# A decoder trunk on one core: group 0's values in two passes, compression adds on GpSimd, another order of blocks, maxima ahead of exponentials

## The chip, the core and the metric

The kernel runs on one core of a Trainium2 chip. Its engines are TensorE (PE, with PEld for its weight loads), VectorE (DVE), ScalarE (ACT), GpSimd (POOL) and SyncE (SP), which issues the DMAs. The metric is the device time of one execution in microseconds (us); lower is better. The times of the kernel before are 1174.12, 1171.5 and 1175.63, median 1174.12.

## What is computed

A trunk of two layers over 512 tokens of width 1024, in f32. Layer 1 is a retention layer, followed by a gated per-layer embedding. From its output one norm and one projection give the keys and values that layer 2 attends to, and a small MLP compresses 32 tokens at a time to one compressed key and value per group. Layer 2 is attention of 16 query heads in four groups: over the compressed positions (31 of them), over selected blocks and over a window. With 512 tokens the selection takes every block and the window covers all, so these two are full causal attentions. The three results are mixed by sigmoid gates, multiplied by a SiLU gate and projected.

```python
def compress_blocks(a, pe, w1, w2):
    sub = a.reshape(b, g, t // CMP_STRIDE, CMP_STRIDE, d)
    blocks = jnp.concatenate([sub[:, :, o:o + n_cmp] for o in range(lc)], axis=3)
    blocks = (blocks + pe).reshape(b, g, n_cmp, CMP_LEN * d)
    return jax.nn.gelu(blocks @ w1) @ w2
...
    s_c = jnp.einsum('bgrqd,bgnd->bgrqn', q, k_cmp) * scale
    p_c = jnp.where(valid_c, jax.nn.softmax(jnp.where(valid_c, s_c, NEG), axis=-1), 0.0)
...
    return gates[..., 0:1] * o_c + gates[..., 1:2] * o_s + gates[..., 2:3] * o_w
```

## The kernel before

Every f32 product is made of three matmuls on rounded operands: each operand is split into a high half (a ScalarE copy to the rounded type) and a low half (a VectorE subtraction), and `mm3` issues high x high, high x low and low x high. The schedule is written by hand: each engine executes its instructions in the order in which the code issues them, and the framework adds only the waits. A tile of PSUM that two engines use is handed over in that order too.

**Weights** come as a stream of pieces (class `Stream`), in the order that `order()` writes out, through four raw buffers and six slots for split pieces. `low` (L205) makes the low half of the oldest piece on VectorE and then issues on SP the DMA that reuses its raw buffer, four pieces ahead. `high` (L190) makes a high half on ScalarE when a slot is free. `mul` (L176) multiplies norm gains into a raw piece on GpSimd, two instructions for each q or k piece and none for the pieces of the compression weights (wk, wv). `tick` does low, high, mul once or twice, and is called from all over the kernel; `get` makes sure that the next piece is ready, and `done` frees its slot.

**Start.** 24 matmuls on zeros (L327) run ahead of the first projection, whose first operands come from ScalarE L136 and L389 and VectorE L137 and L390.

**Group 0's values.** `v_proj(0, t)` multiplies the normed rows of token tile t with three pieces (`kvb`, together 8 k-steps of 304 columns) into one PSUM bank and splits the result into v2H and v2L; the last 48 columns become the branch gates. The four tiles go one after the other, with the transposes of the last row block (`to_aT(3)`) between the second and the third.

**Compression.** `compress(b)`, b = 0 for keys and 1 for values, is a generator. `block(s)`, for s = 0 to 7, adds the position embedding to every 16th column of the projected `ckv` (L783, VectorE, 4 x 4 x 31 elements a partition, read with a step of 16), copies the result to a high half (L785, ScalarE), ticks (for s > 1), and makes the low half (L788, VectorE). Step s multiplies blocks s with one piece of wk or wv (12 matmuls of 256 columns) and then issues block(s + 2). After step 7 come a Gelu, two transposes with a split, and the second layer (w2). Compression of the keys is interleaved with the projections c_proj(1, g), that of the values with the query projections `q_proj(0, h)`: two steps after each of the first three queries, then steps 6 and 7 in a row, then the fourth query. The first key projection, the w2 layer of the values, the first scores and the second key projection follow (L1012 to L1019).

**Scores.** `scores(g, u)` serves unit u of a group (u = 2h for selection, 2h + 1 for the window, of head h). It fills three PSUM banks, for row block 3, row block 2 and row blocks 0 and 1; per bank VectorE adds the causal mask and then, per row block, takes the maximum (L944), after which ScalarE takes the exponential with a running sum (L945). In even units the compressed positions' scores stand in the same banks; `cmp_probs` adds their mask (L883) after all banks and goes on with their softmax. Between units `pair_tile` adds output tiles to the residual (L1006) and `probs_T` transposes probabilities and splits them (L364, L365).

Of the kernel before, what the change touches and what calls it, by code (L numbers as in the profile page):

```python
# [47 lines left out]
def order():  # L48
# [26 lines left out]
    def kk(g):  # L75
        return [("kv", 0, 1024, b + 128 * g, 128) for b in (1024, 1536)]
# [4 lines left out]
    def q(g):  # L81
        return [("nin", 0, 1024, 512 * g + 128 * h, 128) for h in range(4)]
# [6 lines left out]
    for n, dense in (("wk", [("kv", 0, 1024, 512 + 128 * g, 128) for g in range(4)]),  # L89
                     ("wv", q(0)[:3])):  # L90
        o += [("w2", 0, 512, 0, 128)] if n == "wv" else []
        for i, d in enumerate(dense):
            o += [d] + [(n, 512 * (2 * i + e), 512, 0, 256) for e in (0, 1)]
    o += [("wv", 512 * i, 512, 0, 256) for i in (6, 7)] + [q(0)[3]] + kk(0)
# [142 lines left out]
def decoder(ctx: ExitStack, tc: tile.TileContext, x, xT, stream, cst, msk, gains, fnorm, out):  # L237
# [88 lines left out]
    for i in range(24):  # L326
        pe.matmul(o[:, :256], masks[:, :128], masks[:, :256], start=True, stop=True)  # L327
# [146 lines left out]
    def run(g):  # L474
        for _ in g:
            pass
# [228 lines left out]
    def v_proj(g, t, p, bank="d", tick=True):  # L705
        n = 256 if g else 304
        o = psum(bank)[:, :n]
        k0 = 0
        for q in p:
            m = q.h.shape[1]  # L710
            mm3(o, [(aH[:, t, k0 + k], aL[:, t, k0 + k], q.h[:, k], q.l[:, k])
                    for k in range(m)], k0 == 0, k0 + m == NK)
            k0 += m
        split_psum(v2H[:, t], v2L[:, t], o[:, :256])
        if g == 0:
            act.activation(bg[:, t], o[:, 256:], AF.Tanh, scale=0.5)
        if tick:
            W.tick()
        if t == 3:
            for q in p:  # L720
                q.done()
# [53 lines left out]
    def compress(b):  # L775

        def block(s):
# [5 lines left out]
            dve.tensor_add(B[:, :, :, :31], src,  # L783
                           pos[:, :, None, None].to_broadcast([128, 4, 4, 31]))
# [54 lines left out]
    v_proj(0, 0, p, "d", False)  # L839
    v_proj(0, 1, p, "o", False)  # L840
    to_aT(3, hn[1])
    v_proj(0, 2, p, "d", False)
    W.tick(1)
    v_proj(0, 3, p, "s")
# [13 lines left out]
    for h in range(3):  # L858
        f = q_proj(0, h)
        next(f)  # L860
        if h < 2:
            next(comp)
        run(f)
        next(comp1)
        next(comp1)
    next(comp1)
    next(comp1)
    f = q_proj(0, 3)
    next(f)
    act.activation(small[:, 250:251], half, AF.Exp)  # L870
    next(comp1)
    run(f)
# [6 lines left out]
    def cmp_probs(g, h, banks):  # L879

        q, q4 = pc[h % 2], pc4[h % 2]
        for i, o in banks:
            dve.tensor_add(q[:, i:i + 2], o, cmask[:, i:i + 2])  # L883
# [24 lines left out]
    def scores(g, u):  # L908
# [4 lines left out]
        cmp = []  # L913
# [5 lines left out]
        for bank in ((3,), (2,), (0, 1)):  # L919
# [8 lines left out]
            if e and 2 in bank:  # L928
                block(o[:, 416:448], 3, 0, 32)
                cmp.append((2, o[:, 0:448].rearrange("p (a n) -> p a n", a=14)[:, 0:14:13]))  # L930
            elif e and 0 in bank:
                cmp.append((0, o[:, 0:480].rearrange("p (a n) -> p a n", a=3)[:, 0:2, :32]))
# [8 lines left out]
            for i, f in zip(bank, at):  # L941
                n = 128 * i + 128
                w = o[:, f:f + n]
                dve.reduce_max(mx[:, i:i + 1], w, axis=mybir.AxisListType.X, negate=True)  # L944
                act.activation(Pu[:, PO[i]:PO[i] + n], w, AF.Exp, bias=mx[:, i:i + 1],  # L945
                               accum_out=sm_[:, i:i + 1])
        chain = cmp_probs(g, h, cmp) if e else iter(())
# [63 lines left out]

    k_proj(0, 0)  # L1012
    next(comp1)
    w2p.done()
    dve.tensor_scalar(bg, bg, 0.5, 0.5, op0=OP.mult, op1=OP.add)
    sums, chain = scores(0, 0)
    scale_probs(0, 0, sums)
    run(chain)
    k_proj(0, 1)  # L1019
# [155 lines left out]
```

## Time and profile before

| | |
|---|---|
| median of the three runs | 1174.12 us |
| the profiled execution, its own time | 1176.46 us |
| its span, first to last instruction | 1174.7 us |
| mean granted TensorE clock | 0.988 |
| busy: PE, PEld | 1140.1 us, 970.0 us |
| busy: DVE, ACT, POOL | 727.8, 490.8, 294.9 us |
| HBM read, written | 98.83 MB, 2.10 MB |

Busy time says how much of the span an engine worked; an idle engine that nobody waits for costs nothing. [...] In a timeline a line stands for a run of like instructions, and the brackets hold the engine's idle time ahead of it and the instruction that ended this.

### The profile page before, as it was taken

Reading aid. Unit: us, or ns where it says so; the run is one execution under the profiler, and the core shown is the slowest. Engines: PE = TensorE matmul, PEld = TensorE weight load, DVE = VectorE, ACT = ScalarE, POOL = GpSimd, SP = SyncE. Lnnn points to the kernel's source line nnn. Section 1 sums busy time; section 2 is a strip of 40 time slices with the busy share of each in tenths; the row PEclk is TensorE's granted clock in tenths of the full one; section 3 lists DMA queues with packets and bytes.
Section 4 is the critical chain, followed back from the end, with each engine's and each line's share of the span. In section 5 each row is a group of like instructions: output and inputs, shape, how many; then the busy total and the mean of one; then the engine's idle time right before and its main releaser. Section 6 shows DMA issues by size and latency. Waiting matters only on the chain. (4 is left out here: it accounts for less than half of the span.)

```text
span 1174.7 us, 15278 instructions
## 1 busy us (share of the span) xinstructions
PE 1140.1 (97%) x5806; PEld 970.0 (83%) x5806; DVE 727.8 (62%) x1242; ACT 490.8 (42%) x916; POOL 294.9 (25%) x341
## 2 busy tenths in 40 slices
PE   8999999999999999899699999999999999999997
PEld 7888888888888888888587888888898888887886
DVE  4746336544534556467857764778468774787555
ACT  6333233232323445345446443444344533444653
POOL 0212003002100222223435331454243431321012
PEclk9999999999999999999799999999999999999999
DMA  8422321322232131255512201221121211221211
GB/s 326 141 97 72 111 96 54 93 95 72 90 108 90 54 124 39 83 152 175 149 69 73 73 21 51 73 74 56 50 91 54 73 54 41 86 77 50 72 37 71
DMA packets 29593, 101.90 MB, mean 87 GB/s; under 512 B 3536, under 2 KB 3792, under 8 KB 29520
## 3 DMA queue, kind: packets, MB, share of 16 engines
q1 hardware_dynamic: 29088, 100.15, 26.2%
q8 instruction: 45, 0.74, 0.3%
q10 hardware_dynamic: 432, 0.79, 0.2%
q14 instruction: 28, 0.23, 0.1%
HBM read 98.83 MB, written 2.10 MB: 86 GB/s over the span
## 5 line engine op out<-in xcount | busy, mean ns | idle before, releaser
L355 PE MATMUL d<-arenaR 128*128 128x512 f32 (+2 forms) x2904 | 678.1, 386 | 10.4 <-DVE arenaF L1006 3.6
L355 PEld LDWEIGHTS d<-arenaR 128*128 128x128 f32 x2904 | 525.6, 189 | 113.9 <-DVE arenaF L1006 5.5
L355 PE MATMUL s<-arenaR 128*128 128x512 f32 (+8 forms) x1182 | 239.5, 353 | 0.2 <-DVE arenaR L829 0.2
L205 DVE TENSOR_TENSOR arenaR<-arenaF,arenaR 128x1024 fp32r<-128x1024 f32 (+1 forms) x142 | 194.1, 1386 | 66.1 <-ACT arenaR L190 66.0
L355 PEld LDWEIGHTS s<-arenaR 128*128 128x128 f32 x1182 | 200.3, 188 | 29.8 <-DVE arenaR L829 0.3
L190 ACT ACTIVATE arenaR<-arenaF 128x1024 fp32r<-128x1024 f32 (+1 forms) x142 | 145.8, 1048 | 104.4 <-PE s L355 68.4
L176 POOL TENSOR_TENSOR arenaF<-arenaF 128x512 f32<-128x512 f32 x108 | 137.0, 1291 | 126.2 <-DMA arenaF<-stream_dram 126.1
L355 PE MATMUL o<-arenaR 128*128 128x512 f32 (+3 forms) x744 | 133.4, 331 | 11.0 <-DVE arenaR L788 5.0
L355 PEld LDWEIGHTS o<-arenaR 128*128 128x128 f32 x744 | 119.1, 198 | 24.0 <-DVE arenaR L788 5.8
L958 POOL TENSOR_SCALAR arenaF<-arenaF 128x512 f32<-128x512 f32 (+3 forms) x128 | 66.8, 541 | 254.1 <-ACT arenaR L364 120.1
L945 ACT ACTIVATE arenaF<-s,arenaF 128x512 f32<-128x512 f32 (+3 forms) x128 | 67.6, 528 | 102.9 <-DVE arenaF L944 100.2
L365 DVE TENSOR_TENSOR arenaR<-pt,arenaR 128x512 fp32r<-128x512 f32 (+1 forms) x141 | 82.8, 617 | 35.5 <-ACT arenaR L364 33.8
L364 ACT ACTIVATE arenaR<-pt 128x512 fp32r<-128x512 f32 (+1 forms) x141 | 70.7, 540 | 80.0 <-PE pt L967 40.4
L371 POOL TENSOR_TENSOR arenaF<-arenaF 128x1 f32<-128x1 f32 (+1 forms) x25 | 14.2, 568 | 294.7 <-DVE arenaF L370 294.7
L944 DVE TENSOR_REDUCE arenaF<-s 128x1 f32<-128x512 f32 (+3 forms) x128 | 62.9, 491 | 22.2 <-ACT arenaF L945 18.9
L355 PE MATMUL pt<-arenaR 128*128 128x512 f32 (+1 forms) x384 | 75.9, 349 | 0.0
L355 PEld LDWEIGHTS pt<-arenaR 128*128 128x128 f32 x384 | 62.7, 188 | 9.4
L209 DVE SCALAR_TENSOR_TENSOR arenaR<-arenaF,arenaR 128x512 fp32r<-128x512 f32 x64 | 45.7, 762 | 35.0 <-PE pt L355 21.4
L194 ACT ACTIVATE arenaR<-arenaF 128x512 fp32r<-128x512 f32 x64 | 43.1, 721 | 46.6 <-issue 22.3
L967 PEld LDWEIGHTS pt<-arenaF 128*128 128x128 f32 x318 | 38.4, 141 | 12.1 <-DVE arenaR L365 4.5
L967 PE MATMUL pt<-arenaF 128*128 128x128 f32 x318 | 45.1, 273 | 3.2 <-DVE arenaR L365 3.2
L1006 DVE TENSOR_TENSOR arenaF<-arenaF,d 128x512 f32<-128x512 f32 x64 | 41.8, 682 | 7.0 <-PE d L355 6.7
(126 smaller groups left out, 692.6 us busy)
## 6 DMA issues: line engine op xcount, KB each, us to landing
arenaF<-stream_dram SPq DMA_DIRECT2D x174, 512.0 KB, 3.5
arenaF<-xT_dram SPq DMA_DIRECT2D x8, 256.0 KB, 5.0
arenaF<-x_dram SPq DMA_DIRECT2D x4, 512.0 KB, 8.3
out_dram<-arenaF SPq DMA_DIRECT2D x3, 512.0 KB, 2.6
arenaF<-cst_dram SPq DMA_DIRECT2D x4, 256.0 KB, 3.8
arenaF<-stream_dram ACTq DMA_DIRECT2D x2, 256.0 KB, 4.4
arenaF<-stream_dram SPq DMA_DIRECT2D x2, 256.0 KB, 6.0
arenaF<-cst_dram SPq DMA_DIRECT2D x1, 512.0 KB, 9.9
```

What stands on the lines that cost most here:

```text
L176: self.nc.gpsimd.tensor_mul(r3[:, k], r3[:, k], g[:, k, None].to_broadcast([128, m // 2, w]))
L190: self.nc.scalar.activation(hi[:, :m * w], raw, AF.Copy)
L194: self.nc.scalar.activation(hi[:, c], raw[:, c], AF.Copy, scale=g[:, k:k + 1])
L205: self.nc.vector.tensor_sub(lo[:, :m * w], raw, hi[:, :m * w])
L209: self.nc.vector.scalar_tensor_tensor(lo[:, c], raw[:, c], g[:, k:k + 1], hi[:, c], op0=OP.mult, op1=OP.subtract)
L355: pe.matmul(o, a, b, start=start and i == 0, stop=stop and i == n - 1)
L364: act.activation(h, src, AF.Copy)
L365: dve.tensor_sub(l, src, h.bitcast(F32))
L944: dve.reduce_max(mx[:, i:i + 1], w, axis=mybir.AxisListType.X, negate=True)
L945: act.activation(Pu[:, PO[i]:PO[i] + n], w, AF.Exp, bias=mx[:, i:i + 1], accum_out=sm_[:, i:i + 1])
L958: pool.tensor_scalar(w, w, sm_[:, i:i + 1], 1.0, op0=OP.mult, op1=OP.mult)
L967: pe.transpose(p[:, f:f + 128], Pu[:, PO[i] + 128 * j:PO[i] + 128 * j + 128], ident)
```

## The change

Six edits, in the order of the diff:

- `order()` puts the fourth query piece, q(0)[3], between the sixth and the seventh wv piece, where it stood behind the eighth.
- The warm-up has 30 matmuls for 24.
- `v_proj` is divided: `v_sums` does the matmuls of given pieces into a given bank. Tiles 0, 1 and 2 of group 0 are first summed over pieces one and two, with the transposes of the last row block ahead of tile 2; then piece three is added to each and its result split; tile 3 comes last.
- The position add of `block(s)` is issued on GpSimd instead of VectorE.
- The driver of group 0 follows the new order of pieces: step 6 of the values' compression comes in the middle of the fourth query's projection and step 7 after it. The transposes follow the first key projection, the w2 layer follows the second, and the first scores stand between the two.
- In `scores` all maxima of a bank come ahead of its exponentials, and the add of the compressed positions' mask (earlier in `cmp_probs`) comes between them.

```diff
--- before.py
+++ after.py
@@ -87,11 +87,11 @@
     o += [("kvb", r, min(384, 1024 - r), 0, 304) for r in (0, 384, 768)]
     o += [("kv", 0, 1024, 128 * g, 128) for g in range(4)]
     for n, dense in (("wk", [("kv", 0, 1024, 512 + 128 * g, 128) for g in range(4)]),
-                     ("wv", q(0)[:3])):
+                     ("wv", q(0))):
         o += [("w2", 0, 512, 0, 128)] if n == "wv" else []
         for i, d in enumerate(dense):
             o += [d] + [(n, 512 * (2 * i + e), 512, 0, 256) for e in (0, 1)]
-    o += [("wv", 512 * i, 512, 0, 256) for i in (6, 7)] + [q(0)[3]] + kk(0)
+    o += kk(0)
 
     def block(kind, g, i):
         if kind == "emb":
@@ -323,7 +323,7 @@
 
     pool.memset(masks[:, :256], 0.0)
     o = psum("o")
-    for i in range(24):
+    for i in range(30):
         pe.matmul(o[:, :256], masks[:, :128], masks[:, :256], start=True, stop=True)
     for k in range(NK):
         nc.sync.dma_start(rx[:, k], xT[k // 2, :, 512 * (k % 2):512 * (k % 2) + 512])
@@ -702,15 +702,19 @@
     blk = [V(fb + 6144 + 512 * i, 512) for i in range(2)]
     hid = V(fb, 256)
 
-    def v_proj(g, t, p, bank="d", tick=True):
-        n = 256 if g else 304
-        o = psum(bank)[:, :n]
-        k0 = 0
+    def v_sums(t, o, p, k0):
         for q in p:
             m = q.h.shape[1]
             mm3(o, [(aH[:, t, k0 + k], aL[:, t, k0 + k], q.h[:, k], q.l[:, k])
                     for k in range(m)], k0 == 0, k0 + m == NK)
             k0 += m
+
+    def v_proj(g, t, p, bank="d", tick=True, o=None):
+        if o is None:
+            o = psum(bank)[:, :256]
+            v_sums(t, o, p, 0)
+        else:
+            v_sums(t, o, p[2:], 6)
         split_psum(v2H[:, t], v2L[:, t], o[:, :256])
         if g == 0:
             act.activation(bg[:, t], o[:, 256:], AF.Tanh, scale=0.5)
@@ -780,8 +784,8 @@
             src = bass.AP(tensor=src.tensor, offset=src.offset + 4 * s,
                           ap=[list(src.ap[0]), [1, 4], [512, 4], [16, 31]])
             pos = gn[:, (G_PEV if b else G_PEK) + 4 * s:][:, :4]
-            dve.tensor_add(B[:, :, :, :31], src,
-                           pos[:, :, None, None].to_broadcast([128, 4, 4, 31]))
+            pool.tensor_add(B[:, :, :, :31], src,
+                            pos[:, :, None, None].to_broadcast([128, 4, 4, 31]))
             act.activation(bkH[s % 4], blk[s % 2], AF.Copy)
             if s > 1:
                 W.tick()
@@ -836,12 +840,17 @@
     ple_gate(0, norm_rows, norm_T)
     p = v_pieces(0)
     W.tick(1)
-    v_proj(0, 0, p, "d", False)
-    v_proj(0, 1, p, "o", False)
+    o = [psum(bank)[:, :304] for bank in ("d", "o", "d", "s")]
+    v_sums(0, o[0], p[:2], 0)
+    v_sums(1, o[1], p[:2], 0)
     to_aT(3, hn[1])
-    v_proj(0, 2, p, "d", False)
+    v_sums(2, o[2], p[:2], 0)
+    v_proj(0, 0, p, tick=False, o=o[0])
+    v_proj(0, 1, p, tick=False, o=o[1])
     W.tick(1)
-    v_proj(0, 3, p, "s")
+    v_proj(0, 2, p, tick=False, o=o[2])
+    v_sums(3, o[3], p[:2], 0)
+    v_proj(0, 3, p, o=o[3])
     for i in range(2):
         dve.memset(blk[i], 0.0)
     for g in range(4):
@@ -855,32 +864,27 @@
     w2p = W.get("w2", 0, 512, 0, 128)
     comp1 = compress(1)
     next(comp1)
-    for h in range(3):
+    for h in range(4):
         f = q_proj(0, h)
         next(f)
         if h < 2:
             next(comp)
+        if h == 3:
+            next(comp1)
         run(f)
         next(comp1)
-        next(comp1)
-    next(comp1)
-    next(comp1)
-    f = q_proj(0, 3)
-    next(f)
+        if h < 3:
+            next(comp1)
     act.activation(small[:, 250:251], half, AF.Exp)
-    next(comp1)
-    run(f)
 
     tri = masks[:, M_TRI:M_TRI + 128]
     cmask = masks[:, M_CMP:M_CMP + 128].rearrange("p (i n) -> p i n", i=4)
     PO = [896, 1024, 512, 0]
     TO = [0, 512, 1024, 896]
 
-    def cmp_probs(g, h, banks):
+    def cmp_probs(g, h):
 
         q, q4 = pc[h % 2], pc4[h % 2]
-        for i, o in banks:
-            dve.tensor_add(q[:, i:i + 2], o, cmask[:, i:i + 2])
         mx, sm_ = scal(4), scal(4)
         dve.reduce_max(mx, q, axis=mybir.AxisListType.X)
         dve.tensor_sub(q, q, mx[:, :, None].to_broadcast([128, 4, 32]))
@@ -910,7 +914,6 @@
         Pu = P[u % 2]
         e = 0 if b else 32
         mx, sm_ = scal(4), scal(4)
-        cmp = []
 
         def block(w, i, lo, hi):
             c = slice(128 * i, 128 * i + 128)
@@ -927,9 +930,11 @@
                 f += n
             if e and 2 in bank:
                 block(o[:, 416:448], 3, 0, 32)
-                cmp.append((2, o[:, 0:448].rearrange("p (a n) -> p a n", a=14)[:, 0:14:13]))
+                cmp = 2, o[:, 0:448].rearrange("p (a n) -> p a n", a=14)[:, 0:14:13]
             elif e and 0 in bank:
-                cmp.append((0, o[:, 0:480].rearrange("p (a n) -> p a n", a=3)[:, 0:2, :32]))
+                cmp = 0, o[:, 0:480].rearrange("p (a n) -> p a n", a=3)[:, 0:2, :32]
+            else:
+                cmp = None
             if 1 in bank:
 
                 d = bass.AP(tensor=o.tensor, offset=o.offset + e,
@@ -939,12 +944,16 @@
                 d = o[:, at[0] + 128 * bank[0]:][:, :128]
                 dve.tensor_add(d, d, tri)
             for i, f in zip(bank, at):
+                dve.reduce_max(mx[:, i:i + 1], o[:, f:f + 128 * i + 128],
+                               axis=mybir.AxisListType.X, negate=True)
+            if cmp:
+                i, d = cmp
+                dve.tensor_add(pc[h % 2][:, i:i + 2], d, cmask[:, i:i + 2])
+            for i, f in zip(bank, at):
                 n = 128 * i + 128
-                w = o[:, f:f + n]
-                dve.reduce_max(mx[:, i:i + 1], w, axis=mybir.AxisListType.X, negate=True)
-                act.activation(Pu[:, PO[i]:PO[i] + n], w, AF.Exp, bias=mx[:, i:i + 1],
+                act.activation(Pu[:, PO[i]:PO[i] + n], o[:, f:f + n], AF.Exp, bias=mx[:, i:i + 1],
                                accum_out=sm_[:, i:i + 1])
-        chain = cmp_probs(g, h, cmp) if e else iter(())
+        chain = cmp_probs(g, h) if e else iter(())
         next(chain, 0)
         return sm_, chain
 
@@ -1009,14 +1018,15 @@
         for kind, *i in (b for h in range(4) for b in between(g, h)):
             yield from {"gate": g_proj, "q": q_proj, "nout": pair_tiles, "emb": emb_tiles}[kind](*i)
 
+    dve.tensor_scalar(bg, bg, 0.5, 0.5, op0=OP.mult, op1=OP.add)
     k_proj(0, 0)
     next(comp1)
-    w2p.done()
-    dve.tensor_scalar(bg, bg, 0.5, 0.5, op0=OP.mult, op1=OP.add)
     sums, chain = scores(0, 0)
     scale_probs(0, 0, sums)
+    k_proj(0, 1)
+    next(comp1)
+    w2p.done()
     run(chain)
-    k_proj(0, 1)
 
 
     PLAN = [3, 3, 2, 1, 2, 3, 2, 2]
```

## Rows read from the trace of the kernel before

**Rows 1.** Page, parts 1 and 6: busy us (share); issues, KB, us to landing
```profile
PE 1140.1 (97%) x5806; PEld 970.0 (83%) x5806; DVE 727.8 (62%) x1242; ACT 490.8 (42%) x916; POOL 294.9 (25%) x341
...
arenaF<-stream_dram SPq DMA_DIRECT2D x174, 512.0 KB, 3.5
```

**Rows 2.** Timeline, TensorE, start: start, us, instruction, count, [idle, releaser]
```profile
1.09 4.94 PE L327 MATMUL o<-masks 128*128 128x256 bf16 x24 [1.09 <-POOL masks L324]
7.94 13.19 PE L355 MATMUL d<-arenaR 128*128 128x512 f32 x48 [1.92 <-ACT arenaR L136]
20.97 11.04 PE L355 MATMUL s<-arenaR 128*128 128x512 f32 x48
```

**Rows 3.** Windows: stretch, length, busy us by engine, granted clock, DMA, GB/s
```profile
8.96:12.38 3.42, 3.42 (x9) 2.65 (x10) 3.42 (x6) 3.42 (x7) 0.00 (x0) 0.51 1.02 364
555.00:570.00 15.00, 13.90 (x82) 12.14 (x81) 12.12 (x14) 8.33 (x13) 1.84 (x2) 1.00 0.64 202
575.78:589.10 13.32, 8.93 (x31) 7.62 (x32) 9.99 (x7) 6.38 (x8) 9.93 (x8) 0.50 0.55 158
```

**Rows 4.** Timeline, TensorE, values of group 0
```profile
475.30 0.96 PE L355 MATMUL d<-arenaR 128*128 128x304 f32 x5 [3.35 <-DVE arenaR L205]
476.10 5.04 PE L355 MATMUL o<-arenaR 128*128 128x304 f32 x24
...
485.21 3.52 PE L355 MATMUL s<-arenaR 128*128 128x304 f32 x24
```

**Rows 5.** Timeline, VectorE, the same stretch
```profile
473.62 2.76 DVE L205 TENSOR_TENSOR arenaR<-arenaF,arenaR 128x608 fp32r<-128x608 f32 x2
```

**Rows 6.** Waits of TensorE: line, releaser, us in total, times, longest
```profile
PE o L355 <- DVE arenaR L788: 5.0, 3, 3.1
PE o L355 <- ACT arenaR L785: 4.7, 1, 4.7
PE d L355 <- DVE arenaF L1006: 3.6, 8, 0.9
...
PE o L355 <- DVE arenaR L365: 0.8, 1, 0.8
```

**Rows 7.** Timeline, TensorE, compression of the values
```profile
549.41 3.04 PE L355 MATMUL o<-arenaR 128*128 128x256 f32 x24
...
577.90 3.15 PE L355 MATMUL o<-arenaR 128*128 128x256 f32 x12 [0.80 <-DVE arenaR L788]
584.11 2.50 PE L355 MATMUL o<-arenaR 128*128 128x256 f32 x10 [3.06 <-DVE arenaR L788]
586.41 4.22 PE L355 MATMUL d<-arenaR 128*128 128x512 f32 x12
```

**Rows 8.** One line, L783: min/median/max ns, first and last start
```profile
L783 DVE TENSOR_TENSOR arenaF<-arenaF x16: 969/1006/1802, 511.2 to 577.8; 128x496 f32<-128x496 f32 x16
```

**Rows 9.** Timeline, GpSimd, gains multiplied into weight pieces
```profile
479.05 2.04 POOL L176 TENSOR_TENSOR arenaF<-arenaF 128x512 f32<-128x512 f32 x2 [4.45 <-DMA arenaF<-stream_dram]
...
568.15 5.46 POOL L176 TENSOR_TENSOR arenaF<-arenaF 128x512 f32<-128x512 f32 x4 [14.30 <-DMA arenaF<-stream_dram]
```

**Rows 10.** Timeline, VectorE, low halves of weight pieces
```profile
558.16 1.22 DVE L205 TENSOR_TENSOR arenaR<-arenaF,arenaR 128x1024 fp32r<-128x1024 f32 x1
...
570.72 3.98 DVE L205 TENSOR_TENSOR arenaR<-arenaF,arenaR 128x1024 fp32r<-128x1024 f32 x2
```

**Rows 11.** Timeline, ScalarE, compression of the values
```profile
575.62 0.63 ACT L785 ACTIVATE arenaR<-arenaF 128x512 fp32r<-128x512 f32 x1 [4.60 <-DVE arenaF L783]
576.16 1.04 ACT L190 ACTIVATE arenaR<-arenaF 128x1024 fp32r<-128x1024 f32 x1
```

**Rows 12.** Timeline, VectorE, split of the first k projection
```profile
599.69 0.69 DVE L365 TENSOR_TENSOR arenaR<-d,arenaR 128x512 fp32r<-128x512 f32 x1 [4.75 <-ACT arenaR L364]
```

**Rows 13.** Timeline, VectorE, one of the scores with compression
```profile
755.92 0.42 DVE L944 TENSOR_REDUCE arenaF<-s 128x1 f32<-128x256 f32 x1 [0.58 <-ACT arenaF L945]
...
756.97 0.23 DVE L883 TENSOR_TENSOR arenaF<-s,masks 128x64 f32<-128x64 f32 x1 [0.50 <-ACT arenaF L945]
```

## The prediction

> **What bounds the kernel now.** I read the page's first part first: TensorE is busy in 97% of the span and no other engine above 62% [rows 1]. So a change pays only where TensorE waits or where its clock is low, and I list these places: the waits of PE by releaser, its timeline around each, and the stretches at half clock. The idle column of the other engines tells nothing by itself; GpSimd and ScalarE wait most of the time and cost nothing. Four places bear on this change.
>
> *Start.* The 24 warm-up matmuls end at 6.03, the first real one starts at 7.94, 1.92 us later, released by ScalarE [rows 2]. [...] The first 48 matmuls take 13.19, the next 48 of the same shape 11.04 [rows 2].
>
> *Values of group 0.* TensorE waits 3.35 us at 475.30 for the low half of the third weight piece (L205), then runs 24 matmuls in 5.04 where the same 24 take 3.52 ten microseconds later [rows 4]; the clock had fallen again. VectorE does that low half at 473.62, behind the norm of the last row block [rows 5].
>
> *Compression of the values.* From 561 to 584 TensorE waits for blocks of compression input: 5.0 us in three waits for their low halves (L788) and 4.7 in one for a high half (L785) [rows 6]. From 575.78 to 589.10 the clock is 0.50 [rows 3]: 12 + 10 matmuls of 256 columns take 3.15 + 2.50 and 12 of 512 take 4.22, against 3.04 for 24 of the first kind [rows 7] and 11.04/4 = 2.76 for the second [rows 2]. That is 9.87 - (2.79 + 2.76) = 4.3 us of slow work. Lost in all: 9.7 + 4.3 = 14.0.
>
> *Attention.* Eight waits for L1006 sum to 3.6, the longest 0.9, and one for L365 on the accumulator is 0.8 [rows 6]; both are adds or splits that queue on VectorE behind the work of the scores.
>
> **The change part by part**, against the profiled run's own 1176.46 us (span 1174.7, 1.8 around it). The three runs shown have a median 2.3 us lower; a low-clock stretch costs 1.5 to 2 us, so one or two fewer of these would explain it, and part of what I count below may already be missing there. I therefore take the sum from 1176.46 and don't subtract the 2.3 again.
>
> *A, warm-up, 6 more matmuls.* 24 take 4.94, so six take at most 1.24 and end by 7.27, still before the 7.94 at which ScalarE's high half is ready; they delay nothing. The idle time shrinks to 0.7 us or a little more. From 555 to 570 TensorE is idle for 1.1 us and the clock stays at 1.00 [rows 3]; the waits of 1.92 [rows 2] and 3.35 [rows 4] were followed by the low level. So I expect no fall. Worth: at most 13.19 - 11.04 = 2.15; but part of the 13.19 is waiting for inputs that arrive one by one, which a faster clock doesn't shorten, so I take 1.5. Bounds 0 and 2.1.
>
> *B, values in two passes.* TensorE first sums pieces one and two for token tiles 0, 1 and 2, and only then needs piece three. Where it stood still it now has 18 matmuls of tile 1 (18 x 3.52/24 = 2.6), the eight transposes (0.8) and 18 of tile 2 (2.6): 6.0 us of cover against 3.35. The normed rows that the transposes need leave VectorE just before 473.62 and TensorE comes to them at about 474.4, so no wait replaces the old one; without the wait the clock stays up. Evacuations move back by the same few microseconds; the first to need their bank is the projection that follows, three tiles later. Worth 3.35 + 1.52 = 4.9, less 0.2 of ends: 4.7. Bounds 3.3 and 4.9.
>
> *C, q(0)[3] ahead of the last two wv pieces, and the adds on GpSimd.* The 16 adds take VectorE 1.0 each [rows 8]. GpSimd's nearest row is a 128x512 multiply, 1.02 each alone (2.04 for two) and 1.37 when VectorE runs beside it (5.46 for four) [rows 9]. No row shows GpSimd reading with a step of 16 elements, as this add does. Bounds 1.0 and 2.2 (1.37 stretched as far as VectorE's low half is when the two meet, 1.99 for 1.22 [rows 10]); I take 1.4, since VectorE is busy beside most of these adds. [...]
>
> What matters more is GpSimd's order. It also multiplies gains into every q and k piece, and each multiply waits for its DMA: 14.30 us before 568.15 [rows 9]. By the order of issue the multiply for q(0)[3] now stands ahead of the add of block 4, that for the first k piece ahead of block 6, that for the second ahead of block 7; ScalarE's copy, its next high half and VectorE's next low half queue behind each add, and that low half frees the buffer for the DMA after next. One turn of this ring: landing 3.5 [rows 1], multiplies 2.04, add 1.4, copy 0.63, high half 1.04 [rows 11], low half 1.22 [rows 10] = 9.8. TensorE needs one turn for each q piece with two wv pieces: 24 x 11.04/48 + 3.04 = 8.6. The ring loses 1.2 to 1.3 a turn; it starts with block 2 ready about 2.8 us before its use, so blocks 2 to 5 come in time (0.3 for wv4), and after three turns wv6 waits about 3.9 - 2.8 = 1.1, with the low half following 0.4 later: 1.5. The second half of q(0)[3] (2.76) then runs, and wv7 waits for block 7, whose low half stands behind the low half of the first k piece: multiplies, add, copy, high, low and subtract after 573.6 give 581.3, TensorE is there at 579.3 or so: 1.7 as a mean with an uncontended GpSimd.
> Without q(0)[3] in that place both waits would be 2.76 longer; it is the cover, and its own low half (issued one turn earlier now) is ready just as wv5 ends.
> The second k projection and the second layer of the value compression (w2) move behind the first scores. So those scores follow the first k projection directly, with two transposes (0.4) between: they need ScalarE's and VectorE's split of it, a copy of 512 columns on ScalarE, 0.63 [rows 11], and the subtract on VectorE, 0.69 [rows 12], so 1.3 - 0.4 = 0.95 of new wait with the hand-overs. The w2 matmuls lose nothing, since the softmax of the first scores runs beside them. VectorE's own relief (16 x 1.0) is partly eaten: its low half takes 1.99 instead of 1.22 while GpSimd works [rows 10].
> New waits: 0.3 + 1.5 + 1.7 + 0.95 = 4.4, and 1.2 for one more low-clock stretch that is not sure. C = 14.0 - 5.6 = 8.4. With adds of 1.0 the waits are about 2.5 (C = 11.5); with 2.2 each turn loses 0.8 more, three turns ahead of wv6, one ahead of wv7, some at wv1, and C = 4.6.
>
> *D, maxima ahead of exponentials.* VectorE stood still 0.58 before the last maximum and 0.50 before the second compression add, each time until an exponential was done [rows 13]. With both maxima and the adds ahead of the exponentials these 1.08 us go in each of the 16 units that have compression scores; ScalarE's last exponential ends some 0.3 earlier. In the other 16 only ScalarE's end counts, 0.2 or less as I step through it, which I leave out. So the L1006 waits beside such units (all but the last, 0.3: 3.3 us, each under 0.9) and the 0.8 of L365 vanish but for 0.1. TensorE is the bound there, so what it no longer waits is gained. D = 4.0, bounds 1 and 5.5. The exponentials that start later by an add (0.2) wait for nobody: VectorE's reciprocal behind them is still earlier.
>
> Sum: 1.5 + 4.7 + 8.4 + 4.0 = 18.6, so 1176.46 - 18.6 = 1157.9.
>
> **The rivals.**
> *1. GpSimd is the late one.* Adds of about 2.2, or copies that queue longer than I step through: C = 4.6, time 1161.7, and with a low clock in the longer waits 1163. For it: the multiply that waits for DMA stands ahead of the add. Against: GpSimd is idle over half of that stage. [...] Chance 0.17.
> *2. The small parts do little.* The clock falls at the start all the same, and the L1006 waits turn into waits for the next instruction: A = 0, D = 1, time 1162.4. Chance 0.10.
> *3. The change doesn't relieve VectorE.* GpSimd's adds hold back VectorE's low halves (1.22 to 1.99) as much as they take off it; of C only q(0)[3]'s cover is left, 2 x 2.76: 1160.8, and up to 1165 with the low clock as it was. Chance 0.06.
> *4. Slower.* One mechanism: the strided add on GpSimd costs so much that GpSimd becomes the bound of the compression stage. From the first add at 511.2 to the end of the last, 577.8 + 1.0 [rows 8], lie 67.6 us; GpSimd would do 16 adds and, for seven pieces, 14 multiplies at 1.37, 19 us. A + B + D give 10.2, so the kernel loses from 16p + 19 > 77.8, p above 3.7 us, over three times its nearest row. At p = 4: 1176.46 + 83 - 77.8 = 1181.7. Chance 0.04.
> *5. Better.* Adds of 1.0 and no new low clock: C = 11.5 and D = 5.5, time 1153.3. Chance 0.08.
>
> **How the numbers follow.** The forecast's own case, 1154 to 1161, has 0.55. Range 1151 to 1166: it takes in rivals 1, 2, 5 and most of 3. A difference under 0.3% (3.5 us) can't be told from none here; only the far ends of 1 and 3 land there: 0.03. Slower 0.04, faster 0.93.
>
> **What would show it.** A: clock 1.00 from 8 to 13 and the first 48 matmuls in under 12. B: no wait of PE for L205, the values done in 15 us from their first matmul. C: waits of PE for L785 or L788 near wv6 and wv7 of 1 to 2 each, a new one for L365 of about 0.9 ahead of the first scores, GpSimd's add between 1.0 and 1.5 alone. D: the waits for L1006 nearly gone. Wrong if GpSimd's adds take over 2 us, if VectorE is as full as before in that stage, or if the clock falls in more places than before.

## The result and the profile after

| | before | changed |
|---|---|---|
| median, us | 1173.59 (1171.5 to 1175.63, 4 runs) | 1155.37 (1155.29 to 1155.66, 4 runs) |
| profiled execution, its own time | 1176.46 | 1155.31 |
| its span, granted clock | 1174.7, 0.988 | 1153.3, 0.997 |

The ratio is 0.9845, 95% interval 0.9827 to 0.9863: 18.2 us faster. The time lies 2.5 us under the forecast of 1157.9 and inside its own case. Two of the sum's four terms were wrong, and their errors partly cancelled.

To see where time went, I cut the span at four instructions of TensorE that every version issues, and read their start in the timeline: the second 48 matmuls of 512 columns (end of the start), the first matmul of c_proj (values done), the first matmul with 96 rows (compression and the first scores done) and the end. The distances between them need no idle column. All kernels of the experiments are in the table, one profiled execution each:

| kernel | start | to c_proj | to the 96-row matmul | to the end |
|---|---|---|---|---|
| before | 20.97 | 467.59 | 142.04 | 544.1 |
| changed | 19.48 | 462.51 | 136.41 | 534.9 |
| changed, again | 18.58 | 462.54 | 136.01 | 534.8 |
| scores as before | 18.52 | 462.47 | 136.52 | 543.5 |
| pieces as before | 19.00 | 462.50 | 142.04 | 534.8 |
| adds on VectorE | 21.21 | 462.47 | 136.03 | 534.5 |
| values in one pass | 18.84 | 468.67 | 136.46 | 534.6 |
| 24 warm-up matmuls | 19.28 | 462.46 | 136.13 | 534.6 |
| adds ahead; again | 18.89; 18.34 | 462.49; 462.49 | 133.70; 135.46 | 534.6; 534.6 |
| adds ahead, on VectorE | 19.06 | 462.48 | 132.07 | 534.4 |
| adds ahead, w2 first | 19.20 | 462.52 | 138.56 | 536.9 |
| adds ahead, scores cleared | 18.32 | 462.46 | 132.23 | 534.5 |
| the same, on VectorE | 19.16 | 462.45 | 132.83 | 534.5 |

From before to changed the steps give A 1.5, B 5.1, C 5.6 and D 9.2, together 21.4, the difference of the spans. Forecast were 1.5, 4.7, 8.4 and 4.0, together 18.6. The medians differ by 18.2 only, since the profiled execution of the kernel before was 2.9 us longer than its median. That 18.2 is so near the 18.6 is luck; the four steps gave 2.8 more than the sum.

The start and the values, which answer to [rows 2, 4]: the timeline of TensorE in the changed kernel (start, us, instruction, count, idle before and its releaser).

```profile
1.08 5.83 PE L327 MATMUL o<-masks 128*128 128x256 bf16 x30 [1.08 <-POOL masks L324]
7.95 11.70 PE L355 MATMUL d<-arenaR 128*128 128x512 f32 x48 [1.03 <-ACT arenaR L136]
...
467.62 2.76 PE L355 MATMUL d<-arenaR 128*128 128x304 f32 x18
...
473.54 3.60 PE L355 MATMUL d<-arenaR 128*128 128x304 f32 x24
```

The first real matmul starts where it did (7.94 before), but the 48 take 11.70 for 13.19. In the values no wait is left; from 467.62 to c_proj at 481.99 they take 14.4.

The compression of the values, which answers to [rows 6, 7]: the same view.

```profile
563.27 2.89 PE L355 MATMUL o<-arenaR 128*128 128x256 f32 x22 [1.39 <-DVE arenaR L792]
566.00 2.91 PE L355 MATMUL d<-arenaR 128*128 128x512 f32 x12
570.52 0.50 PE L355 MATMUL o<-arenaR 128*128 128x256 f32 x2 [1.61 <-ACT arenaR L789]
571.41 1.56 PE L355 MATMUL o<-arenaR 128*128 128x256 f32 x10 [0.38 <-DVE arenaR L792]
572.77 4.43 PE L355 MATMUL d<-arenaR 128*128 128x512 f32 x12
...
579.05 1.46 PE L355 MATMUL o<-arenaR 128*128 128x256 f32 x10 [1.61 <-DVE arenaR L792]
...
586.67 0.50 PE L355 MATMUL s<-arenaR 128*128 128x512 f32 x1 [0.47 <-ACT arenaR L364]
587.39 2.38 PE L355 MATMUL s<-arenaR 128*128 128x512 f32 x14 [0.22 <-DVE arenaR L365]
```

The prediction's names hold: wv4 is step 4 of this compression, the one that waits 1.39 here; wv6 waits 1.61 + 0.38 and wv7 1.61. With two smaller ones ahead (0.52 and 0.21) these are eight waits of 6.4 together, where before had four of 9.7 [rows 6]. The 12 matmuls at 572.77 take 4.43 where the 12 at 566.00 take 2.91: the clock had fallen. The granted clock, the third number from the end, in the windows that answer to [rows 3] (1.00 is full speed; in half-microsecond windows from 470 to 482 the kernel before shows 1.00 or 0.50, and 0.55 and 0.53 in the two where it changes):

```profile
8.96:12.38 3.42, 3.42 (x15) 2.66 (x16) 3.42 (x6) 3.42 (x7) 0.00 (x0) 1.00 1.00 336
...
572.50:576.00 3.50, 3.50 (x12) 2.82 (x11) 0.84 (x1) 1.50 (x3) 3.50 (x3) 0.52 0.37 130
```

The start is at 1.00 now, where it was 0.51; the low stretch in the compression is this one, at 0.52.

GpSimd in that stage, which answers to [rows 9]: gains (L176) and adds (L787) in one queue.

```profile
566.19 2.40 POOL L176 TENSOR_TENSOR arenaF<-arenaF 128x512 f32<-128x512 f32 x2 [5.19 <-DMA arenaF<-stream_dram]
568.55 1.26 POOL L787 TENSOR_TENSOR arenaF<-arenaF 128x496 f32<-128x496 f32 x1
569.77 2.49 POOL L176 TENSOR_TENSOR arenaF<-arenaF 128x512 f32<-128x512 f32 x2
572.22 2.25 POOL L787 TENSOR_TENSOR arenaF<-arenaF 128x496 f32<-128x496 f32 x1
```

The order is the one stepped through in the prediction: each add stands behind the gains of a query or key piece, and these wait for a DMA.

### The profile page after: what moved, and what is told of

Same layout as the page of the kernel before. It is cut to its first block, busy times and chain, and to the rows that moved or that the text cites. A ratio compares the mean times of both kernels' runs of the same rounds, so it can differ in the third digit from the quotient of the medians.

```text
span 1153.3 us, 15259 instructions
## 1 busy us (share of the span) xinstructions
PE 1132.1 (98%) x5812; PEld 964.3 (84%) x5812; DVE 710.4 (62%) x1226; ACT 486.7 (42%) x916; POOL 317.4 (28%) x357
## 5 line engine op out<-in xcount | busy, mean ns | idle before, releaser
L205 DVE TENSOR_TENSOR arenaR<-arenaF,arenaR 128x1024 fp32r<-128x1024 f32 (+1 forms) x142 | 191.7, 1369 | 70.5 <-ACT arenaR L190 70.3
L176 POOL TENSOR_TENSOR arenaF<-arenaF 128x512 f32<-128x512 f32 x108 | 135.3, 1276 | 99.2 <-DMA arenaF<-stream_dram 94.7
L355 PE MATMUL o<-arenaR 128*128 128x512 f32 (+3 forms) x744 | 128.8, 322 | 6.3 <-DVE arenaR L792 4.1
L355 PEld LDWEIGHTS o<-arenaR 128*128 128x128 f32 x744 | 114.3, 189 | 19.6 <-DVE arenaR L792 5.1
L365 DVE TENSOR_TENSOR arenaR<-pt,arenaR 128x512 fp32r<-128x512 f32 (+1 forms) x141 | 82.9, 618 | 36.9 <-ACT arenaR L364 34.3
L209 DVE SCALAR_TENSOR_TENSOR arenaR<-arenaF,arenaR 128x512 fp32r<-128x512 f32 x64 | 45.7, 763 | 35.1 <-PE pt L355 21.4
L947 DVE TENSOR_REDUCE arenaF<-s 128x1 f32<-128x512 f32 (+3 forms) x128 | 59.9, 489 | 3.3
```

Source lines behind the costliest of these rows:

```text
L176: self.nc.gpsimd.tensor_mul(r3[:, k], r3[:, k], g[:, k, None].to_broadcast([128, m // 2, w]))
L205: self.nc.vector.tensor_sub(lo[:, :m * w], raw, hi[:, :m * w])
L209: self.nc.vector.scalar_tensor_tensor(lo[:, c], raw[:, c], g[:, k:k + 1], hi[:, c], op0=OP.mult, op1=OP.subtract)
L355: pe.matmul(o, a, b, start=start and i == 0, stop=stop and i == n - 1)
L365: dve.tensor_sub(l, src, h.bitcast(F32))
L947: dve.reduce_max(mx[:, i:i + 1], o[:, f:f + 128 * i + 128], axis=mybir.AxisListType.X, negate=True)
```

## The experiments

Diffs are against the changed kernel; three dots mark lines left out. Each ratio is to the kernel before, timed beside that run. The changed kernel's second timing gave 1154.45 (1153.66 to 1155.48), ratio 0.9835 (0.9808 to 0.9861):

> The changed kernel itself, beside the others on this chip: 1155.4, with one stretch of low clock near 573 or none; if that stretch is chance, some execution has it elsewhere or not at all.

### What the maxima are worth

```diff
             for i, f in zip(bank, at):
-                dve.reduce_max(...)
-            if cmp: ...
-            for i, f in zip(bank, at):
+                dve.reduce_max(...)
                 act.activation(... AF.Exp ...)
```

> The changed kernel with the order of maxima, exponentials and compression add as before. If a wait of TensorE costs what the idle column shows, 4.0 to 4.5 us are lost: 1159.4 to 1159.9. If each costs some 0.3 more than the column shows, and the low clock near the third unit comes back, 8 to 9.5: 1163.4 to 1164.9.

Measured 1163.43 (1162.75 to 1165.03), ratio 0.9907 (0.9892 to 0.9922): 8 to 9 us, against 4.0 forecast. The waits of TensorE by releaser (us, times, longest):

```profile
PE d L355 <- DVE arenaF L1012: 3.7, 8, 0.9
PE pt L973 <- DVE arenaR L365: 3.7, 4, 1.6
```

In the changed kernel the first are 0.3 in one wait and the second 1.9 in three:

```profile
PE pt L976 <- DVE arenaR L365: 1.9, 3, 1.1
...
PE d L355 <- DVE arenaF L1015: 0.3, 1, 0.3
```

On VectorE the two stops that the prediction named [rows 13] are gone as well; the maxima and the mask's add follow each other without one:

```profile
739.61 0.62 DVE L947 TENSOR_REDUCE arenaF<-s 128x1 f32<-128x128 f32 x2
740.15 0.21 DVE L951 TENSOR_TENSOR arenaF<-s,masks 128x64 f32<-128x64 f32 x1
```

So the waits forecast to vanish did, yet 8.6 us of the last stage hang on this order. The low clock near the third unit did not come back here (four transposes behind the wait of 1.55 at 629.74 take 0.61, as in the changed kernel; the kernel before has 1.05, behind a wait of 1.80), so it is not what costs: TensorE's idle time in this stage is 9.9 against 4.1, and the other 2.8 stand in no idle column. One place shows why. TensorE before:

```profile
757.05 1.03 PE L967 MATMUL pt<-arenaF 128*128 128x128 f32 x8
758.50 3.02 PE L355 MATMUL d<-arenaR 128*128 128x512 f32 x12 [0.41 <-DVE arenaF L1006]
```

and in the changed kernel:

```profile
741.49 1.03 PE L976 MATMUL pt<-arenaF 128*128 128x128 f32 x8
742.28 3.00 PE L355 MATMUL d<-arenaR 128*128 128x512 f32 x12
```

From the eight transposes to the next run it is 1.45 with the wait and 0.79 without: 0.66 lost where the idle column says 0.41. Without a wait the next run starts 0.24 ahead of the end that the trace gives for the one before (1.03 after a start that is 0.79 earlier); with a wait this overlap is lost too and counted as busy. Five waits of before show 0.41 each; between the nearest matmuls of the compressed positions on either side of one (the 96-column transposes ahead, the 96-row matmul behind), the changed kernel is 0.68 to 0.74 shorter, 0.71 in the mean, so 0.30 more than the column shows.

### What the order and the adds on GpSimd are worth

First the pieces in the old order, with the adds still on GpSimd:

```diff
-                     ("wv", q(0))):
+                     ("wv", q(0)[:3])):
...
-    o += kk(0)
+    o += [("wv", 512 * i, 512, 0, 256) for i in (6, 7)] + [q(0)[3]] + kk(0)
```

with steps 6 and 7 in a row ahead of the fourth query.

> The changed kernel with the fourth query piece behind the eighth wv piece, as before. If its 2 x 2.76 us of cover is what shortens the waits at wv6 and wv7: 5 to 6 us slower, 1160.5 to 1161.5, more with a longer low clock. If the adds on GpSimd had already cured those waits: 1155 to 1157.

Measured 1160.75 (1160.41 to 1161.58), ratio 0.9884 (0.9867 to 0.99). Its stage takes 142.04, as before (to the hundredth by chance: profiles of one order differ by up to 0.5 there), with nearly the same waits as [rows 6], 4.4 for 4.7 and 3.1 for 3.1:

```profile
568.86 3.39 PE L355 MATMUL o<-arenaR 128*128 128x256 f32 x12 [4.42 <-ACT arenaR L789]
573.51 0.80 PE L355 MATMUL o<-arenaR 128*128 128x256 f32 x2 [1.26 <-ACT arenaR L789]
577.37 2.50 PE L355 MATMUL o<-arenaR 128*128 128x256 f32 x10 [3.06 <-DVE arenaR L792]
```

In the old order, then, the move to GpSimd gains nothing, nor does the new place of the transposes and the w2 layer, which this run keeps; the new order of pieces makes all of C. The other way round, the new order with the adds on VectorE:

```diff
-            pool.tensor_add(B[:, :, :, :31], src,
+            dve.tensor_add(B[:, :, :, :31], src,
```

> The changed kernel (1155.4) with the position adds back on VectorE, all else as changed. Theory (ring): the waits at wv4, wv6 and wv7 come from GpSimd's order, where an add stands behind a multiply that waits for its DMA; then these waits shrink from 5.0 us in all to under 3 and the time is 1152 to 1155. Rival (VectorE load): VectorE is what is late, its 16 us of adds come back and the waits grow; the time is 1157 to 1161.

Measured 1154.31 (1153.74 to 1155.99), ratio 0.983 (0.9815 to 0.9844), and 136.03 for the stage: the same. The ring theory had the waits right: at wv4, wv6 and wv7 they fall from 5.0 to 2.4.

```profile
572.32 0.50 PE L355 MATMUL o<-arenaR 128*128 128x256 f32 x2 [1.72 <-ACT arenaR L789]
...
579.50 1.45 PE L355 MATMUL o<-arenaR 128*128 128x256 f32 x10 [0.25 <-DVE arenaR L792]
```

But the stage does not get shorter. TensorE now waits 0.63 for the low half of q(0)[3] and 0.61 for GpSimd ahead of the first scores, and the clock is low behind wv6 here too (0.79 from 571 to 579). VectorE's busy time from 497 to 580 is 67.3, with the adds on GpSimd it is 50.4 (496 to 580). VectorE is relieved by 17 us, and the time is the same.

The second run of the changed kernel shows what holds the last block:

```profile
571.47 2.91 PE L355 MATMUL d<-arenaR 128*128 128x512 f32 x12
...
577.83 1.45 PE L355 MATMUL o<-arenaR 128*128 128x256 f32 x10 [3.22 <-DVE arenaR L792]
```

Here the clock stays up (granted 1.00 from 555 to 590), the 12 matmuls take 2.91, and the wait for block 7 is 3.22, not 1.61. Counted from c_proj the block is there after 96.7 us in the one and 97.1 in the other (577.83 - 481.12; 579.05 - 481.99). In these two executions the chain that feeds the block sets the time, and the low clock ahead of it cost next to nothing.

If the place in the queue is the cause and not the engine, adds issued earlier must gain. Four block buffers, and the add of block s + 4 right after step s:

```diff
-    blk = [V(fb + 6144 + 512 * i, 512) for i in range(2)]
+    blk = [V(fb + 6144 + 512 * i, 512) for i in range(4)]
...
+        for s in range(4):
+            add(s)
...
+            if s < 4:
+                add(s + 4)
             if s < 6:
                 block(s + 2)
```

> The changed kernel with four input buffers for the compression blocks, so that each add is issued on GpSimd two steps earlier, ahead of the multiplies that wait for DMA. Ring theory: the waits at wv4 and wv6 go, the low clock after them too, wv7's shrinks: 1149 to 1151.5. If VectorE or the landing of the weights is late, not the add: 1154 to 1156.

> The adds issued ahead, a second time beside the two others: 1151.5 to 1153.6 as before. If it comes out at 1154 or above, the gain of 2 to 3 us over the changed kernel was chance.

Measured 1152.60 (1151.53 to 1153.6), ratio 0.9813 (0.9798 to 0.9827), and again 1152.21, ratio 0.9811 (0.9795 to 0.9827): 2 to 3 us better by the medians. The gain is small beside the spread: the intervals overlap with that of the changed kernel's second timing, and the stage of the second run is only 0.6 to 1.0 shorter; but no execution of the two runs was above 1153.6, and none of the changed kernel below 1153.66. The ring theory's 1149 to 1151.5 was not reached. The waits for wv4, wv6 and wv7 are gone; one of 0.85 stands at an earlier step (0.21 in the changed kernel), and ahead of the first scores come 2.7 us (3.5 in the second; 0.7 in the changed kernel), with matmuls at low clock behind them (0.70 from 585 to 589, and 6.65 for 24 where the changed kernel has 5.63):

```profile
579.93 0.50 PE L355 MATMUL s<-arenaR 128*128 128x512 f32 x1 [0.84 <-ACT arenaR L364]
581.51 0.73 PE L355 MATMUL s<-arenaR 128*128 128x512 f32 x2 [1.09 <-DVE arenaR L365]
582.97 2.53 PE L355 MATMUL s<-arenaR 128*128 128x416 f32 x12 [0.72 <-POOL arenaR L764]
585.30 6.65 PE L355 MATMUL d<-arenaR 128*128 128x512 f32 x24
```

The same with the adds on VectorE (`dve.tensor_add`):

> As the run with the adds issued ahead, but the adds on VectorE. Theory: the place of the adds (GpSimd or VectorE) is worth nothing by itself, only where they stand in the queue; with the adds early both engines have the time, so 1152 to 1154, as with GpSimd. Rival: VectorE, which has 16 us more to do between 505 and 578, becomes the late one again and the low halves of the pieces wait behind the adds: 1155 to 1158.

Measured 1152.17 (1150.46 to 1152.87), ratio 0.9809 (0.9792 to 0.9826): no difference. The instructions by line and shape from 497 to 580 (busy, mean ns, idle before) show why VectorE has no less to do with the adds on GpSimd (66.6 us busy; 64.5 with the adds on VectorE). With the adds on GpSimd:

```profile
L205 DVE TENSOR_TENSOR arenaR<-arenaF,arenaR 128x1024 fp32r<-128x1024 f32 x26 | 44.1, 1716 | 8.4 <-ACT arenaR L190 8.3
...
L787 POOL TENSOR_TENSOR arenaF<-arenaF 128x496 f32<-128x496 f32 x16 | 28.8, 1825 | 0.1
...
L794 DVE TENSOR_TENSOR arenaR<-arenaF,arenaR 128x512 fp32r<-128x512 f32 x16 | 20.9, 1310 | 7.5 <-ACT arenaR L791 7.3
```

and on VectorE:

```profile
L205 DVE TENSOR_TENSOR arenaR<-arenaF,arenaR 128x1024 fp32r<-128x1024 f32 x26 | 36.9, 1439 | 11.8 <-ACT arenaR L190 11.8
...
L787 DVE TENSOR_TENSOR arenaF<-arenaF 128x496 f32<-128x496 f32 x16 | 15.9, 1031 | 3.3 <-ACT arenaF L775 3.3
...
L794 DVE TENSOR_TENSOR arenaR<-arenaF,arenaR 128x512 fp32r<-128x512 f32 x16 | 13.3, 843 | 0.0
```

Of the 15.9 us taken off VectorE 14.8 come back, 7.2 in L205 and 7.6 in the blocks' low halves, while GpSimd is busy for 62.8 of these 83 us; with the adds on VectorE it is for 36.0. That holds for the early adds: in the changed kernel L205 takes 1433 ns in the mean, against 1504 with the adds on VectorE, and the blocks' low halves 987 against 794, so only 3 us come back there.

### What stands ahead of the first scores

On top of the adds ahead, the w2 layer ahead of the first scores, with the transposes in the middle of the first key projection:

```diff
-    k_proj(0, 0)
+    k_proj(0, 0, lambda: next(comp1))
     next(comp1)
+    w2p.done()
     sums, chain = scores(0, 0)
...
-    next(comp1)
-    w2p.done()
```

> The kernel with the adds issued ahead, and besides the two transposes of the value compression in the middle of the first key projection and its second layer ahead of the first scores. If the wait of 0.5 + 0.2 ahead of the first scores is a cost on the path: 0.7 to 1.3 less than with the adds ahead alone, 1148 to 1150.5. If those matmuls are missed later, ahead of the first transposes of probabilities: no difference.

Measured 1157.98 (1155.83 to 1159.03), ratio 0.9858 (0.9826 to 0.9891): about 5 us worse than without this edit, where a gain or no difference was expected.

```profile
582.21 0.44 PE L355 MATMUL s<-arenaR 128*128 128x128 f32 x2 [2.73 <-ACT arenaR L364]
583.92 9.38 PE L355 MATMUL s<-arenaR 128*128 128x128 f32 x37 [1.27 <-DVE arenaR L365]
```

w2 now waits 4.0 for the split of its input, and then runs at the lower clock (0.50 from 584 to 593); behind it a transpose waits 2.18, where the changed kernel has 1.06. In the change under study the first scores and the second key projection cover that split, as its step C assumed.

So the waits were taken away where the rows put them: VectorE scales the gates (1.09 us) ahead of the split, and GpSimd has ten multiplies ahead of two 32-column copies. Both are moved forward, on top of the adds ahead (`k_cmp` issues the two copies, which `k_proj` issued before):

```diff
     next(comp1)
+    dve.tensor_scalar(bg, bg, 0.5, 0.5, op0=OP.mult, op1=OP.add)
     for h in range(4):
         f = q_proj(0, h)
+        if h == 2:
+            k_cmp(0)
...
-    dve.tensor_scalar(bg, bg, 0.5, 0.5, op0=OP.mult, op1=OP.add)
```

> As the run with the adds issued ahead, and two instructions taken out of the way of the first scores: the gate scaling on VectorE (1.09 us at 579.77, ahead of the split of the first k projection) moves ahead of the query projections, and the two 32-column copies on GpSimd (at 582.71, behind ten multiplies of gains) ahead of the third query. If the waits of 0.84, 1.09 and 0.72 before the first scores are made by what is queued ahead on VectorE and GpSimd, they fall to those of the changed kernel or below (0.47 + 0.22, none for GpSimd), the half-speed matmuls behind them go too (6.65 for 24 becomes 5.63), and the stage from the c_proj matmuls to the first 96x512 matmul takes 131 to 132 where it took 133.7: 1149.9 to 1151.2 against 1152.6. If they are made by ScalarE (the table load, the high halves), they stay and the time is 1152 to 1153.

Measured 1149.39 (1148.76 to 1150.93), ratio 0.9789 (0.9772 to 0.9806): this version beats both kernels, the changed one by 5 to 6 us.

```profile
573.35 1.46 PE L355 MATMUL o<-arenaR 128*128 128x256 f32 x10 [1.69 <-DVE arenaR L797]
...
581.30 0.49 PE L355 MATMUL s<-arenaR 128*128 128x512 f32 x1 [0.81 <-ACT arenaR L364]
582.03 2.38 PE L355 MATMUL s<-arenaR 128*128 128x512 f32 x14 [0.23 <-DVE arenaR L365]
584.24 5.63 PE L355 MATMUL d<-arenaR 128*128 128x512 f32 x24
```

The wait for GpSimd and the low clock are gone, that for VectorE is 0.23. What ScalarE makes (0.81) stayed, against 0.47 in the changed kernel. In the second run with the adds ahead ScalarE's copy at 580.42 stands right behind the load of an activation table (1.28 from 579.02), which the changed kernel has done 2.8 us before that copy (583.18; 586.02); that this load makes the 0.81 here is the author's estimate. With the adds on VectorE:

> The run with the first scores' queues cleared, but its early adds on VectorE. With the adds on GpSimd, TensorE still waited 1.40 for a low half of a piece (L205) and 1.69 for one of a block (L797), and VectorE's low halves were stretched beside GpSimd's work (VectorE's busy time from 497 to 580 was 66.6 with the adds on GpSimd and 64.5 with them on VectorE itself). If those two waits come from that stretching, they shrink to under 1 each and the time is 1147.5 to 1149; if they come from VectorE's order, where each add would now stand ahead as well, they stay or grow: 1149.5 to 1151.

Measured 1150.14 (1148.02 to 1150.77), ratio 0.9789 (0.9774 to 0.9805), and the two versions can't be told apart. One of the two waits is 0.76 now, at another block, the other is still 1.40, and ScalarE's ahead of the scores is 1.54 for 0.81, with 14 matmuls in 3.95 for 2.38 behind it: the stretching alone is not what holds them.

### Values and warm-up

```diff
-    v_sums(0, o[0], p[:2], 0)
...
+    for t in range(NT):
+        if t == 2:
+            to_aT(3, hn[1])
+        v_sums(t, o[t], p[:2], 0)
+        v_proj(0, t, p, tick=t == 3, o=o[t])
+        if t == 2:
+            W.tick(1)
```

> The changed kernel with group 0's values summed in one pass, tile after tile. If wait, slow clock and the tail of the wait all come back: 5.1 more, 1160.5. If only the wait of 3.35 does: 1158.7.

Measured 1160.23 (1159.46 to 1161.62), ratio 0.9885 (0.9858 to 0.9911). The wait of [rows 4] is back, with low clock behind it (0.58 from 473 to 480); the two passes are worth 5 to 6 us.

```profile
473.23 1.64 PE L355 MATMUL d<-arenaR 128*128 128x304 f32 x5 [3.35 <-DVE arenaR L205]
474.66 5.43 PE L355 MATMUL o<-arenaR 128*128 128x304 f32 x24
```

```diff
-    for i in range(30):
+    for i in range(24):
```

> The changed kernel with 24 warm-up matmuls. If they hold the clock up: the first 48 matmuls take 13.2 us again and the time is 1156.8 (1.4 more). If the clock at the start hangs on when the program starts: no difference, 1155.4.

Measured 1154.72 (1153.85 to 1156.08), ratio 0.9838 (0.9811 to 0.9864): no difference that can be told from none. Its start, with 24:

```profile
1.08 4.56 PE L327 MATMUL o<-masks 128*128 128x256 bf16 x24 [1.08 <-POOL masks L324]
5.91 1.36 PE L355 MATMUL d<-arenaR 128*128 128x512 f32 x3 [0.26 <-ACT arenaR L136]
...
9.85 9.59 PE L355 MATMUL d<-arenaR 128*128 128x512 f32 x41 [0.28 <-DVE arenaR L390]
```

and that of the kernel with adds on VectorE, with 30:

```profile
6.00 2.75 PE L355 MATMUL d<-arenaR 128*128 128x512 f32 x6
...
10.15 11.22 PE L355 MATMUL d<-arenaR 128*128 128x512 f32 x41 [0.28 <-DVE arenaR L390]
```

With 24 the first real matmul started at 5.91, TensorE's waits behind it were 0.32 or less and the clock stayed at 1.00 (from 6 to 20); with 30 it started at 6.00, one wait behind it was 0.62 and the clock still fell (0.58 from 10 to 14). Of the twelve profiled executions with 30 matmuls it fell at the start in this one, of the two with 24 in one, that of the kernel before (0.51 from 8.96 to 12.38).

## Why the prediction was right, and where it wasn't

**A, 1.5.** The profiled pair gave just that (13.19 to 11.70). But the step from pair to cause, that six more matmuls hold the clock up, is not shown: with 24 the second 48 matmuls begin at 19.28, inside the 18.3 to 21.2 of those with 30. The two timings differ by 0.3, and the runs of either spread by 2. What made the clock fall in one execution and not in another, and what six more are worth when the inputs come late, stays open. Rival 2's A = 0 is not excluded.

**B, 4.7.** Right in the mechanism, and a little small: 5.1 between the landmarks, 6.2 in the one profile of the values in one pass, 5 to 6 by the timing, against an upper bound of 4.9. The 6.2 is more than the 5.1 by a longer low clock (0.58 in the seven microseconds from 473, 0.76 in the same seven before): the 5 matmuls behind the wait took 1.64 there for 0.96 before, the next 24 took 5.43 for 5.04. Cover and clock went as worked out, and no wait took the old one's place.

**C, 8.4, measured 5.6.** The cover by q(0)[3] (two times 2.76) was right, and it is all there is, as rival 3 had it: C was 5.5 there. The failed step is the ring's waits: the new waits of 4.4 were 6.4, since wv4 waited 1.39 (0.3 forecast), two earlier steps 0.73 (none) and wv6 1.99 (1.5), against 1.61 for wv7 (1.7) and 0.69 for the first scores (0.95). Eight waits for four also lose four overlaps more, by estimate 0.30 each (0.71 - 0.41) or 1.2, a term that the forecast put at nothing. The estimate for the add was good (1.26 alone, mean 1.53, forecast 1.4) but bought nothing: the stage was no shorter for having GpSimd in the ring. The wait for wv7 and the low clock ahead of it, 1.7 and 1.2 in the forecast, were 1.61 and 1.5 in one execution, 3.22 and none in the other: they make one term of 3.1 to 3.2, well sized, and not two. By these, 14.0 - 6.4 - 1.5 - 1.2 = 4.9, and two small waits of before that were not counted (0.58 and 0.21, now 0.25 and none) give 0.5 more: 5.4, near the 5.6.

**D, 4.0, measured 9.2, beyond the upper bound of 5.5.** The mechanism was right, the size was not. The waits counted, L1006 and L365 on the accumulator, shrank by 4.0 in the idle column, as forecast. Not counted were: the waits of the transposes for L365 and some small ones, 1.3 less; the low clock after the longest of them (0.83 from 640 to 650 before, 1.00 in the changed kernel at the same code), 1.5, since that unit shrank by 2.29 and its wait by 0.74 (1.80 to 1.06); and the overlap lost at each of the seven waits that vanished, by estimate 7 x 0.30 = 2.1. Together 8.9. The failed step is that an idle column was taken for the whole cost of a wait, and that only two kinds of wait were counted; the distance of the same two instructions in a stretch without the wait would have shown it.

**Rivals.** 1 (adds of 2.2) didn't come: 16 adds took 24.2, 1.53 in the mean, the longest 2.29. 2 can't be told from the forecast on the warm-up, and it was wrong on the waits for L1006: 3.6 became 0.3 in one wait, and no other took their place. 3 was right on C, for another reason: in the changed kernel VectorE was relieved and nobody waited for that. 4 is excluded by the same 1.53. 5 gave 1153.3 and had D = 5.5 and C = 11.5; the time came within 2.1 of it by luck, with D larger and C smaller than it had them.

## What to carry to other kernels

A short wait of TensorE cost more here than its idle time in the trace (0.68 to 0.74 for 0.41); price one by the distance between the same instructions with and without it. Before work is moved to another engine, ask whether it is late for its length or for its place in an in-order queue: here moving the adds was worth nothing and issuing them earlier 2 to 3 us, after which the next place in the queues came due and was worth some 3 us more. And an engine that takes over work from VectorE can hand it back as longer instructions: with the early adds on GpSimd 14.8 of 15.9 us came back.

## What the runs showed of the hardware

- Five waits of TensorE in the kernel before, each shown as 0.41, cost 0.68 to 0.74.
- In the changed kernel GpSimd's add with a step of 16 elements (64 bytes) took 1.26 at 568.55, with VectorE idle, for 496 elements a partition, against 1.02 for a multiply of 512 without step [rows 9]: a quarter more an element.
- Instructions of VectorE and GpSimd were longer where the two ran side by side: with the adds ahead, blocks' low halves took 1310 ns in the mean with the adds on GpSimd and 843 with the adds on VectorE; in the changed kernel GpSimd's add took 1.26 to 2.29, 2.25 at 572.22 beside a low half of VectorE that took 1.88 where one at 561.39, with GpSimd idle, took 1.23. What makes them longer is not shown. This is not why the move to GpSimd was worth nothing in the changed kernel: there VectorE was relieved by 17 us all the same.
- With 30 warm-up matmuls the first real matmul started at 5.85 in one execution (adds ahead, scores cleared) and at 7.95 in another (changed), where ScalarE's first copy waited for the DMA of the input until 6.65. The second 48 matmuls began at 18.32 and 19.48: of the 2.1 us 1.2 were left.
